# The first layer's inputs: x and ctx loaded ahead of the weights, the shift chunks taken in pairs, and two projection blocks accumulated tile by tile

## The chip, the cores and the metric

The kernel runs on one core of a Trainium2 chip. The metric is the device time of one execution in microseconds (us), a median over several runs. All times below are microseconds from the start of the profiled execution unless marked otherwise; PE is TensorE, DVE is VectorE, ACT is ScalarE, POOL is GpSimd, SP is SyncE, which here only issues transfers.

## The reference

The whole program is two networks one behind the other (a hybrid of a bidirectional recurrence and attention, MLPs, a state-space mixer, then a second block with three attention branches and a convolutional feed-forward). The change touches only the beginning of the first layer:

```python
mod_l = jnp.split((jax.nn.silu(c) @ ada_w[li] + ada_b[li])[:, None, :], 6, axis=-1)
mod_c = jnp.split(jax.nn.silu(c_ctx) @ ada_w[li] + ada_b[li], 6, axis=-1)
hl = rmsnorm(xl, norm1_g[li]) * (1.0 + mod_l[1]) + mod_l[0]
hc = rmsnorm(xc, norm1_g[li]) * (1.0 + mod_c[1]) + mod_c[0]
...
p_lat = h_lat @ w_in          # hybrid_mixer
p_ctx = h_ctx @ w_in
```

`x` (the latent stream) and `ctx` are 256 tokens by 1024 features each. `mod[0]` is the shift, `mod[1]` the scale; both come from a product of `silu(c)` with the first 2048 columns of `ada_w`.

## The kernel before

Features lie on partitions, tokens on the free axis: `xl` and `xc` are two tiles each of 128 x (4 x 256), and `xk` picks one of the eight k tiles (128 x 256). Both streams stand side by side in tiles of 512 columns, ctx first.

Weights come in blocks of 128 output columns: one load of 512 KB into a `raw` tile (128 x 1024, eight k tiles), issued on SP. A block is split into `whi` (rounded to fp32r, on ACT) and `wlo` (what is left, on DVE), the activation likewise into `hhi` and `hlo`; a projection (`projs`) is 24 matmuls of 512 columns into one PSUM bank: whi with hhi and with hlo for each k, then wlo with hhi for each k.

The modulation's first 16 chunks of 128 columns (`ada`, chunks 0 to 7 the shift, 8 to 15 the scale) are read by `adas`, four at a time: per chunk eight small matmuls against `scc` (the silu of c), then a copy out of PSUM (`adas`), a turn by transposes, a reduce and an add into `mod`.

`mod_act` in its `late` form made the activation: squares of x and ctx on ACT with their sums on PE (`stat`), the inverse root on DVE (`rsq`, ten small steps in a row), `spread` of the factor over the columns on PE, 16 multiplications of x and ctx by it on DVE, then all 16 chunks of `adas`, then for each k tile and stream `f = x*a + b` on DVE, `hhi` on ACT and `hlo = f - hhi` on DVE. With that the projections of the hybrid mixer begin: block 0 (the decay and a inputs), blocks 2 and 3 (the keys, `k`), and so on, each through `shifted`: `pp` copied out of PSUM on ACT, then `sm`, a scaled copy, and a sum on DVE. A second stream, `preps`, is woven between the projections (`weave`), and takes the keys as soon as a block is done.

Engines run their instructions in the order in which the tile framework's scheduler wrote them down; a wait at the head of an engine's queue holds up everything behind it. PSUM is cut into pools of banks by `banks`; `PS_PREP` is two banks of `mm` and six of `w`.

Of the kernel before, what the change touches and what calls it, by code (L numbers as in the profile page):

```python
# [16 lines left out]
T = 256  # L17
# [285 lines left out]
class Kern:  # L303
# [68 lines left out]
    def setup(self):  # L372
        nc, A = self.nc, self.A
        G = self.G = self.pool('G')
        self.ps, self.cut, self.sums, self.late = {}, None, None, []
        self.banks(mm=4, w=4)
        cc = self.tl(G, [128, 8, 2], 'cc')
        nc.sync.dma_start(cc, A['cc'])
        nv = sum(w for _, w in self.vc.values())
# [12 lines left out]
        self.W = self.pool('W')  # L392

    def load_x(self, P, Pc):
        self.xl = [self.tl(P, [128, 4, T], f'xl{i}') for i in range(2)]
# [43 lines left out]
    def projs(self, out, name, b, act, n0, n1):  # L439

        nc = self.nc
        whi, wlo = self.wsplit(self.wraw(name, b))
        ps = self.PSt('mm')[:, :n1 - n0]
        runs = [(w, a, k) for k in range(KT) for w, a in ((whi, act.hi), (whi, act.lo))]
        runs += [(wlo, act.hi, k) for k in range(KT)]
        for i, (w, a, k) in enumerate(runs):
            nc.tensor.matmul(ps, w[:, k], a[k][:, n0:n1], start=i == 0, stop=i == len(runs) - 1)  # L447
            if i % 6 == 5 and i < len(runs) - 1:
                yield 6 * (n1 - n0) / 2400
        out.append(ps)  # L450
        yield 6 * (n1 - n0) / 2400


    def adas(self, chunks, ring=None):

        nc = self.nc
        l = 0
        for b in chunks[::4]:
            ps = self.PSt('mm')
            if b < 16:  # L460
                raws = [self.wraw('ada', b + i, ring=ring) for i in range(4)]
                for i in range(4):
                    for r in range(2):
                        for g in range(4):
                            nc.tensor.matmul(ps[32 * g:32 * g + 32, 128 * i:128 * i + 128],
                                             self.scc[:, 2 * g + r], raws[i][:, 2 * g + r],
                                             start=r == 0, stop=r == 1)
                    yield 0.6
            else:
                raws = [self.wraw('adaw', (b // 4 - 4, g)).rearrange("p k c -> p (k c)") for g in range(4)]  # L470
                for r in range(2):
                    for g in range(4):
                        nc.tensor.matmul(ps[32 * g:32 * g + 32], self.scc[:, 2 * g + r],
                                         raws[g][:, 512 * r:512 * r + 512], start=r == 0, stop=r == 1)
                    yield 0.9
            sb = self.tl(self.W, [128, 512], 'adas', bufs=1)
            nc.scalar.activation(sb, ps, AF.Copy)
            yield 0.1
            pt = self.PSt('w')
            for i in range(4):  # L480
                nc.tensor.transpose(pt[:, 128 * i:128 * i + 128], sb[:, 128 * i:128 * i + 128],
                                    self.C('ident'))
            m = self.mod[l][:, b:b + 4]
            nc.vector.tensor_reduce(m, pt.rearrange("p (c g j) -> p c j g", c=4, g=4)[:, :, 0:2],
                                    AX.X, ADD)
            nc.vector.tensor_tensor(m, m, self.V(f'adab{l}')[:, b:b + 4, None].to_broadcast([128, 4, 2]),
                                    ADD)
            self.mods = b + 4
            yield 0.3

    def ada_rows(self, X):
# [111 lines left out]
            self.spread(pr[:, 128 * t:128 * t + 128], y[:, t:t + 1])  # L603
        return pr

    def mod_act(self, l, which, streams, P, X, mid=None, late=None):


        nc = self.nc
# [4 lines left out]
        pr = self.rms(xs, X, mid)  # L614
        cols = [(i, j, slice(T * i, T * i + T)) for i, j in enumerate(streams)]
        if late:
            for k in range(KT):
                for i, j, s in cols:
                    nc.vector.tensor_tensor(self.xk(xs[i], k), self.xk(xs[i], k), pr[:, s], MUL)
            late()  # L620
        m = 3 * which
        sc = {}
        for j in streams:
# [4 lines left out]
        for k in range(KT):  # L628
            for i, j, s in cols:
                x = self.xk(xs[i], k)  # L630
                a, b = sc[j][:, k:k + 1], self.mod[l][:, 8 * m + k, j:j + 1]
                f = self.tl(X, [128, T], 'mf', bufs=4)
                if late:
                    nc.vector.tensor_scalar(f, x, a, b, op0=MUL, op1=ADD)
                    nc.scalar.activation(hi[k][:, s], x, AF.Identity, scale=a, bias=b)
                    todo.append((lo[k][:, s], f, 0.0, hi[k][:, s]))
                else:
                    nc.vector.scalar_tensor_tensor(f, x, a, pr[:, s], op0=MUL, op1=MUL)
                    nc.scalar.activation(hi[k][:, s], f, AF.Identity, bias=b)
                    todo.append((lo[k][:, s], f, b, hi[k][:, s]))  # L640
# [30 lines left out]

    def hybrid(self):
        nc, A = self.nc, self.A
        R = self.pool('R', side='right')
        self.load_consts(1, R)
        self.Y = self.pool('Y', side='right')
        Hh = self.Hh = self.pool('Hh', side='right')
        X = self.pool('X0')
# [48 lines left out]
        self.R, self.DR = R, DR  # L727
# [1546 lines left out]
```

## Time and profile before

| | |
|---|---|
| median of 3 runs | 2044.55 us (2040.88 to 2045.95) |
| the profiled execution | 2040.4 us, span 2038.6 us |
| PE busy | 1938.1 us, 95% of the span |
| PE weight load busy | 1648.5 us, 81% |
| DVE busy | 1446.8 us, 71% |
| ACT busy | 964.4 us, 47% |
| POOL busy | 149.9 us, 7% |
| chain that ended last, by engine | PE 79%, DVE 8%, DMA 5%, issue 5%, ACT 2%, POOL 1% |

The span is what lies between the first and the last instruction of the profiled execution; its own time is 1.8 us longer. A busy PE counts matmuls whose ends are modelled and overlap, so it is no proof that PE runs at its peak. The part of the program that the change touches is the first 64 us of the span.

### The profile page before, as it was taken

To read this page: it belongs to the slowest core of one execution; us is meant where nothing else is said; L and a number is where in the kernel's file an instruction comes from. 1 tells how busy PE (TensorE), PEld (TensorE's weight loads), DVE (VectorE), ACT (ScalarE), POOL (GpSimd) and SP (SyncE) were. 2 spreads that over 40 slices of the span, in tenths; PEclk is the share of its full clock that TensorE was granted. 3 is DMA by queue.
4 is the path that set the end of the run, shared out by engine and by line. 5 is a ranking of instruction groups with operands and counts; after the bars stand their busy time and mean duration, and the time that the engine had idled before them with its cause. 6 is when DMAs were issued, how large, how long until landed. Compare 5 with 4: busy or idle time off the path is not lost.

```text
span 2038.6 us, 37380 instructions
## 1 busy us (share of the span) xinstructions
PE 1938.1 (95%) x14898; PEld 1648.5 (81%) x14898; DVE 1446.8 (71%) x3044; ACT 964.4 (47%) x1770; POOL 149.9 (7%) x273
## 2 busy tenths in 40 slices
PE   6999799969899999998999999999999999999999
PEld 4776456747698899986778878899986888899999
DVE  4675596696699854437988887666678666667984
ACT  3454233322552434434566665566655445456663
POOL 0022401201031200000000003000000000000000
PEclk8999898989899999999999999999999999999999
DMA  7355843413287853322223325466644323345664
GB/s 274 125 175 203 251 155 120 143 42 124 81 271 243 289 169 93 94 88 71 92 64 86 101 73 158 147 186 185 180 148 153 125 93 115 113 147 173 191 190 150
DMA packets 87021, 299.82 MB, mean 147 GB/s; under 512 B 11213, under 2 KB 14685, under 8 KB 86846
## 3 DMA queue, kind: packets, MB, share of 16 engines
q1 hardware_dynamic: 62064, 221.29, 34.1%
q0 software_dynamic: 20736, 69.64, 10.5%
q10 hardware_dynamic: 4046, 6.49, 1.0%
q8 instruction: 117, 1.92, 0.4%
q14 instruction: 58, 0.48, 0.1%
HBM read 281.63 MB, written 18.90 MB: 147 GB/s over the span
## 4 chain that ended last, share of the span: by engine, by line
PE 79%; DVE 8%; DMA 5%; issue 5%; ACT 2%; POOL 1%; POOLq 0%; SPq 0%; DVEq 0%; ACTq 0%
PE psmm L447 23%; PE psmm L426 11%; PE psmm L429 11%; PE psmm L427 11%; DMA ar<-adat 2%; PE psmm L1635 2%; PE psy L1698 2%; PE psw L524 1%; PE psw L1703 1%; DVE wlo L419 1%; PE psa L429 1%; PE psa L426 1%; PE psa L427 1%; PE pso L2054 1%; PE psya L972 1%
## 5 line engine op out<-in xcount | busy, mean ns | idle before, releaser
L418 ACT ACTIVATE whi<-raw 128x1024 fp32r<-128x1024 f32 x374 | 394.4, 1055 | 482.1 <-PE psmm L427 242.2
L419 DVE TENSOR_TENSOR wlo<-raw,whi 128x1024 fp32r<-128x1024 f32 x374 | 453.5, 1213 | 59.4 <-ACT whi L418 39.1
L447 PE MATMUL psmm<-hhi,whi 128*128 128x256 f32 (+1 forms) x1040 | 337.4, 346 | 6.5 <-ACT whi L418 2.1
L447 PE MATMUL psmm<-hlo,whi 128*128 128x256 f32 (+1 forms) x1040 | 330.9, 339 | 2.1 <-DVE hlo L665 1.5
L426 PE MATMUL psmm<-hhi,whi 128*128 128x258 f32 (+1 forms) x944 | 231.1, 283 | 0.3 <-ACT whi L418 0.3
L427 PE MATMUL psmm<-hlo,whi 128*128 128x258 f32 (+1 forms) x944 | 230.8, 282 | 0.0
L447 PEld LDWEIGHTS psmm<-hhi,whi 128*128 128x128 f32 x1040 | 199.8, 192 | 38.1 <-issue 12.2
L447 PEld LDWEIGHTS psmm<-hlo,whi 128*128 128x128 f32 x1040 | 199.7, 192 | 28.7 <-DVE hlo L663 4.8
L447 PE MATMUL psmm<-hhi,wlo 128*128 128x256 f32 (+1 forms) x1040 | 213.5, 336 | 0.2 <-DVE wlo L419 0.2
L426 PEld LDWEIGHTS psmm<-hhi,whi 128*128 128x128 f32 x944 | 178.7, 189 | 2.7 <-issue 1.4
L427 PEld LDWEIGHTS psmm<-hlo,whi 128*128 128x128 f32 x944 | 179.2, 190 | 0.7 <-issue 0.6
L447 PEld LDWEIGHTS psmm<-hhi,wlo 128*128 128x128 f32 x1040 | 157.4, 189 | 25.1 <-issue 9.1
L426 PE MATMUL psmm<-hi,whi 128*128 128x512 f32 (+1 forms) x512 | 164.0, 340 | 5.3 <-ACT hi L668 5.3
L427 PE MATMUL psmm<-lo,whi 128*128 128x512 f32 (+1 forms) x512 | 161.8, 336 | 0.0
L429 PE MATMUL psmm<-hhi,wlo 128*128 128x258 f32 (+1 forms) x944 | 132.0, 282 | 0.0
L429 PEld LDWEIGHTS psmm<-hhi,wlo 128*128 128x128 f32 x944 | 121.0, 190 | 0.0
L426 PEld LDWEIGHTS psmm<-hi,whi 128*128 128x128 f32 x512 | 96.4, 189 | 19.1 <-ACT hi L668 7.0
L511 DVE SCALAR_TENSOR_TENSOR aj<-ar,cb 128x1024 f32<-128x1024 f32 x80 | 97.8, 1222 | 13.2 <-DMA ar<-adat 10.2
L427 PEld LDWEIGHTS psmm<-lo,whi 128*128 128x128 f32 x512 | 96.3, 189 | 10.3 <-DVE lo L669 0.5
L429 PE MATMUL psmm<-hi,wlo 128*128 128x512 f32 (+1 forms) x512 | 100.0, 338 | 0.0
L1370 ACT ACTIVATE r<-r,s 128x256 f32<-128x256 f32 x96 | 48.9, 510 | 87.8 <-DVE r L1369 87.5
L429 PEld LDWEIGHTS psmm<-hi,wlo 128*128 128x128 f32 x512 | 81.6, 190 | 10.4
(607 smaller groups left out, 3649.0 us busy)
## 6 DMA issues: line engine op xcount, KB each, us to landing
raw<-w SPq DMA_DIRECT2D x128, 512.0 KB, 4.1
ar<-adat POOLq DMA_DIRECT2D x56, 512.0 KB, 4.9
raw<-win SPq DMA_DIRECT2D x55, 512.0 KB, 3.5
raw<-ssdin SPq DMA_DIRECT2D x49, 512.0 KB, 3.6
raw<-hyin SPq DMA_DIRECT2D x26, 512.0 KB, 4.1
raw<-adaw SPq DMA_DIRECT2D x24, 512.0 KB, 5.2
raw<-wg SPq DMA_DIRECT2D x22, 512.0 KB, 3.6
raw<-wu SPq DMA_DIRECT2D x22, 512.0 KB, 3.6
```

Of the source, the lines that this page charges most:

```text
L418: nc.scalar.activation(hi[:, :n], raw, AF.Copy)
L419: nc.vector.tensor_tensor(lo[:, :n], raw, hi[:, :n].bitcast(F32), SUB)
L426: nc.tensor.matmul(ps, whi[:, k], act.hi[k][:, n0:n1], start=start and i == 0, stop=False)
L427: nc.tensor.matmul(ps, whi[:, k], act.lo[k][:, n0:n1], start=False, stop=False)
L429: nc.tensor.matmul(ps, wlo[:, k], act.hi[k][:, n0:n1], start=False, stop=stop and i == len(ks) - 1)
L447: nc.tensor.matmul(ps, w[:, k], a[k][:, n0:n1], start=i == 0, stop=i == len(runs) - 1)
L511: nc.vector.scalar_tensor_tensor(junk, raw, 1.0, cb[j], op0=MUL, op1=MUL, accum_out=self.mod[l][:, b, j:j + 1])
L524: self.nc.tensor.matmul(out[32 * g:32 * g + 32, 128 * b:128 * b + 128], self.C('two' if heads else 'one'), sq, start=start, stop=stop, ski ...
L972: nc.tensor.matmul(pss[h][:, q], bk[r, q], ar[r, q], start=True, stop=True)
L1370: nc.scalar.activation(r[:, s], r[:, s], AF.Relu, bias=sh)
L1635: nc.tensor.matmul(ps, w[:, k0 + k], a[k], start=start and i == 0, stop=stop and i == len(runs) - 1, skip_group_check=True)
L1698: nc.tensor.matmul(o, w[:, q], m[:, q], start=d == 0 and n == 2 and q < 2 and k == 0, stop=k == 1 and d == 1 and n == 3, skip_group_check= ...
```

## The change

x and ctx are now issued first, on ACT's queue, ahead of the vectors and the constants. SP's queue takes the eight scale chunks first, then the weight blocks 0 and 2, then shift chunks with further weight blocks between them. The multiplication by the factor stays on DVE, the 16 `f = x*a + b` go from DVE to POOL, and the shift chunks are taken in pairs: after each pair the parts of its two k tiles are made and both blocks' matmuls of these k tiles (3 products by 2 tiles by 2 blocks) follow. Blocks 0 and 2 are finished in that way and `projs` only hands their PSUM banks over.

```diff
@@ setup
-        self.banks(mm=4, w=4)
+        self.banks(**self.PS_PREP)
         cc = self.tl(G, [128, 8, 2], 'cc')
         nc.sync.dma_start(cc, A['cc'])
...
+        self.load_x(self.X0, self.X0)
@@ wraw
-        raw = self.tl(ring, [128, KT, cols // KT], 'raw0', bufs=8) if ring else \
+        raw = self.tl(ring, [128, KT, cols // KT], f'raw{b // 8}', bufs=4 + b // 8 * 4) if ring else \
@@ projs
+        if (name, b) in self.early:
+            out.append(self.early.pop((name, b)))
+            yield 0.0
+            return
@@ adas
-        for b in chunks[::4]:
-            ps = self.PSt('mm')
+        for b in chunks[::n]:
+            ps = self.PSt('w' if b < 16 else 'mm')
...
+    def first_act(self, P, X, ring):
+        nc = self.nc
+        hi = [self.tl(P, [128, 512], 'hhi', F32R, bufs=KT) for _ in range(KT)]
+        lo = [self.tl(P, [128, 512], 'hlo', F32R, bufs=KT) for _ in range(KT)]
+        cols = [(self.xc, 1, slice(0, T)), (self.xl, 0, slice(T, 512))]
+        pr = self.rms([self.xc, self.xl], X)
+        for k in range(KT):
+            for xs, j, s in cols:
+                nc.vector.tensor_tensor(self.xk(xs, k), self.xk(xs, k), pr[:, s], MUL)
+        drain(self.adas(range(8, 16), ring=ring))
...
+        ws = [self.wsplit(self.wraw('hyin', b)) for b in (0, 2)]
+        pss = [self.PSt('mm') for _ in range(2)]
+        for k0 in range(0, KT, 2):
+            drain(self.adas(range(k0, k0 + 2), ring=ring, n=2))
+            for k in (k0, k0 + 1):
+                for xs, j, s in cols:
+                    x, a, b = self.xk(xs, k), sc[j][:, k:k + 1], self.mod[0][:, k, j:j + 1]
+                    f = self.tl(X, [128, T], 'mf', bufs=4)
+                    nc.gpsimd.tensor_scalar(f, x, a, b, op0=MUL, op1=ADD)
+                    nc.scalar.activation(hi[k][:, s], x, AF.Identity, scale=a, bias=b)
+                    nc.vector.tensor_tensor(lo[k][:, s], f, hi[k][:, s].bitcast(F32), SUB)
+                for (whi, wlo), ps in zip(ws, pss):
+                    for i, (w, a) in enumerate(((whi, hi), (whi, lo), (wlo, hi))):
+                        nc.tensor.matmul(ps, w[:, k], a[k], start=k + i == 0, stop=k == KT - 1 and i == 2)
+        for b, ps in zip((0, 2), pss):
+            self.early['hyin', b] = ps
+        return Act(hi, lo)
@@ hybrid
-        self.load_x(X, X)
-        act = self.mod_act(0, 0, [1, 0], Hh, X, late=lambda: drain(self.adas(range(16), ring=ring)))
+        act = self.first_act(Hh, X, ring)
```

Three places show how the engines' orders move. In all of them a number behind a name tells one tile from another.

The first is DVE, where the factor's inverse root (`rqv`, `rqt`, `rqy`) ends and the multiplications of `xc` and `xl` by the spread factor (`psw_207`) begin. Before:

```order
L562 SCALAR_TENSOR_TENSOR rqv_194<-rqt_196 128x4
L563 SCALAR_TENSOR_TENSOR rqy_195<-rqv_194,rqy_195 128x4
L619 TENSOR_TENSOR xc_103<-xc_103,psw_207 128x256
L619 TENSOR_TENSOR xl_101<-xl_101,psw_207 128x256
L619 TENSOR_TENSOR xc_103<-xc_103,psw_207 128x256
```

Now, with `raw_332` and `raw_338` the loads of blocks 0 and 2:

```order
L571 SCALAR_TENSOR_TENSOR rqv_194<-rqt_196 128x4
L424 TENSOR_TENSOR wlo_335<-raw_332,whi_334 128x1024
L572 SCALAR_TENSOR_TENSOR rqy_195<-rqv_194,rqy_195 128x4
L424 TENSOR_TENSOR wlo_341<-raw_338,whi_340 128x1024
L656 TENSOR_TENSOR xc_83<-xc_83,psw_207 128x256
L656 TENSOR_TENSOR xl_81<-xl_81,psw_207 128x256
```

The splits of two weight blocks now stand between the steps of the root and ahead of the multiplications, so the last step of the root waits for block 0's load.

The second is PE, from the spread of the factor (L568, L577) on. `psw_228` and `psw_278` hold the scale chunks, `psw_346` and `psw_402` the first two pairs of shift chunks, `psmm_344` and `psmm_345` blocks 0 and 2. Before, the spread stood among the chunks:

```order
L568 MATMUL psw_207<-cst_68,rqy_195 128x128 x4
L481 MATMUL psw_271<-cst_68,adas_269 128x128 x4
L465 MATMUL psmm_328<-raw_331,scc_70 32x128 x8
L481 MATMUL psw_321<-cst_68,adas_319 128x128 x4
L465 MATMUL psmm_328<-raw_333,scc_70 32x128 x8
```

Now all the chunks come behind it, and the products of a pair behind the next pair's chunks:

```order
L577 MATMUL psw_207<-cst_91,rqy_195 128x128 x4
L474 MATMUL psw_228<-raw_229,scc_93 32x128 x8
...
L490 MATMUL psw_369<-cst_91,adas_367 128x128 x2
L474 MATMUL psw_402<-raw_403,scc_93 32x128 x8
L474 MATMUL psw_402<-raw_405,scc_93 32x128 x8
L675 MATMUL psmm_344<-hhi_109,whi_334 128x512
L675 MATMUL psmm_345<-hhi_109,whi_340 128x512
L675 MATMUL psmm_344<-hlo_117,whi_334 128x512
...
L675 MATMUL psmm_345<-hhi_110,wlo_341 128x512
L490 MATMUL psw_425<-cst_91,adas_423 128x128 x2
```

The transposes that turn the next pair (`psw_425`) stand behind the twelve products of this pair.

The third is ACT, where blocks 0 and 2 are copied out of PSUM (`pp`) and block 3's weights are rounded (`whi_641`, now `whi_645`). Before:

```order
L713 ACTIVATE pp_592<-psmm_567 128x2x256
L418 ACTIVATE whi_641<-raw_639 128x1024
L418 ACTIVATE whi_679<-raw_677 128x1024
L713 ACTIVATE pp_632<-psmm_607 128x2x256
L747 ACTIVATE wt_540<-wdad_539 64x512
L739 ACTIVATE x_691<-k_541,vec_66 128x512
```

Now:

```order
L742 ACTIVATE pp_627<-psmm_344 128x2x256
L742 ACTIVATE pp_636<-psmm_345 128x2x256
L423 ACTIVATE whi_645<-raw_643 128x1024
L423 ACTIVATE whi_683<-raw_681 128x1024
L776 ACTIVATE wt_614<-wdad_613 64x512
L768 ACTIVATE x_695<-k_615,vec_89 128x512
```

Block 3's weights are now rounded behind both copies. On PE, the statistics of the squared keys (`x_691`, now `x_695`) stood after block 3's twentieth matmul and now stand after its ninth. From block 3's end on, each engine's order is that of before, but for one transpose.

## Rows read from the trace of the kernel before

**Rows 1.** Busy time by stretch: engines' busy time (instructions), granted PE clock, DMA share, GB/s.

```profile
0.00:22.20 22.20, 9.08 (x134) 5.92 (x134) 0.71 (x5) 5.13 (x13) 1.39 (x9) 1.00 0.93 354
39.00:49.20 10.20, 9.29 (x17) 4.70 (x18) 10.20 (x31) 8.06 (x16) 0.25 (x1) 0.50 0.00 1
63.80:140.00 76.20, 76.16 (x362) 57.86 (x361) 54.80 (x112) 37.85 (x63) 14.17 (x34) 1.00 0.42 143
```

**Rows 2.** Transfers of the first 36 us: queues (packets, MB), one issuing line (KB each).

```profile
q10 hardware_dynamic: 1008, 2.88, 22.1%
q0 software_dynamic: 80, 0.26, 1.8%
...
raw<-ada SPq DMA_DIRECT2D x16, 512.0 KB, 9.5
```

**Rows 3.** Timeline, 27 to 36 us: start, duration, engine, line, operation [idle before].

```profile
27.73 0.16 DVE L563 SCALAR_TENSOR_TENSOR rqy<-rqv,rqy 128x4 f32<-128x4 f32 x1
27.94 0.65 PE L568 MATMUL psw<-cst,rqy 128*128 128x128 f32 x4 [1.46 <-DVE rqy L563]
28.69 0.42 DVE L619 TENSOR_TENSOR xc<-xc,psw 128x256 f32<-128x256 f32 x1 [0.80 <-PE psw L568]
29.22 1.08 PE L465 MATMUL psmm<-raw,scc 128*32 128x128 f32 x16
32.84 0.60 ACT L477 ACTIVATE adas<-psmm 128x512 f32<-128x512 f32 x1 [2.85 <-PE psmm L465]
33.49 0.65 PE L481 MATMUL psw<-cst,adas 128*128 128x128 f32 x4 [0.79 <-ACT adas L477]
33.66 0.41 DVE L619 TENSOR_TENSOR xl<-xl,psw 128x256 f32<-128x256 f32 x1
34.08 1.95 PE L465 MATMUL psmm<-raw,scc 128*32 128x128 f32 x64
```

**Rows 4.** Timeline, 37 to 40 us: the first parts of the activation.

```profile
37.73 0.17 DVE L486 TENSOR_TENSOR mod<-mod,vec 128x8 f32<-128x8 f32 x1
38.13 0.60 ACT L635 ACTIVATE hhi<-xc,mod,msc 128x256 fp32r<-128x256 f32 x1 [0.43 <-DVE msc L625]
39.27 0.80 PE L447 MATMUL psmm<-hhi,whi 128*128 128x512 f32 x1 [1.81 <-ACT hhi L635]
```

**Rows 5.** Lines by form, 20 to 50 us: busy us, mean ns of one.

```profile
L663 DVE TENSOR_TENSOR hlo<-mf,hhi 128x256 fp32r<-128x256 f32 x16 | 6.6, 423 | 0.0
...
L418 ACT ACTIVATE whi<-raw 128x1024 fp32r<-128x1024 f32 x2 | 2.1, 1046 | 0.0
...
L419 DVE TENSOR_TENSOR wlo<-raw,whi 128x1024 fp32r<-128x1024 f32 x1 | 1.2, 1228 | 0.0
```

**Rows 6.** Timeline, 48 to 64 us: from the last low-clock products to block 3's end.

```profile
48.26 0.63 PE L447 MATMUL psmm<-hlo,whi 128*128 128x512 f32 x1
48.69 0.59 PE L447 MATMUL psmm<-hhi,whi 128*128 128x512 f32 x1
54.02 0.60 ACT L713 ACTIVATE pp<-psmm 128x512 f32<-128x512 f32 x1 [6.96 <-PE psmm L447]
54.65 0.69 DVE L715 TENSOR_TENSOR sm<-pp 128x512 f32<-128x512 f32 x1 [3.12 <-ACT pp L713]
58.05 0.48 DVE L717 TENSOR_SCALAR k<-pp,omm 128x512 f32<-128x512 f32 x1
59.59 0.75 DVE L718 SCALAR_TENSOR_TENSOR k<-sm,hm,k 128x512 f32<-128x512 f32 x1
61.30 0.41 PE L524 MATMUL psw<-x,cst 128*32 128x128 f32 x4
63.73 0.39 PE L447 MATMUL psmm<-hhi,whi 128*128 128x512 f32 x1
63.96 0.39 PE L447 MATMUL psmm<-hlo,whi 128*128 128x512 f32 x1
```

**Rows 7.** Lines by form of POOL: its only arithmetic on tiles of this size.

```profile
L1317 POOL COPY xc<-df 128x256 f32<-128x256 f32 x4 | 1.5, 406 | 0.0
```

More of the change, by code (lines that the diff above doesn't have):

```diff
@@ L374, in setup @@
         G = self.G = self.pool('G')
-        self.ps, self.cut, self.sums, self.late = {}, None, None, []
-        self.banks(mm=4, w=4)
+        self.ps, self.cut, self.sums, self.late, self.early = {}, None, None, [], {}
+        self.banks(**self.PS_PREP)
         cc = self.tl(G, [128, 8, 2], 'cc')
         nc.sync.dma_start(cc, A['cc'])
+        self.W = self.pool('W')
+        self.R = self.pool('R', side='right')
+        self.Y = self.pool('Y', side='right')
+        self.Hh = self.pool('Hh', side='right')
+        self.X0 = self.pool('X0')
+        self.load_x(self.X0, self.X0)
         nv = sum(w for _, w in self.vc.values())
@@ L391, in setup @@
         nc.gpsimd.memset(self.mod[1], 0.0)
-        self.W = self.pool('W')
     def load_x(self, P, Pc):
@@ L451, in projs, with adas @@
         yield 6 * (n1 - n0) / 2400
-    def adas(self, chunks, ring=None):
+    def adas(self, chunks, ring=None, n=4):
         nc = self.nc
         l = 0
-        for b in chunks[::4]:
-            ps = self.PSt('mm')
+        for b in chunks[::n]:
+            ps = self.PSt('w' if b < 16 else 'mm')
             if b < 16:
-                raws = [self.wraw('ada', b + i, ring=ring) for i in range(4)]
-                for i in range(4):
+                raws = [self.wraw('ada', b + i, ring=ring) for i in range(n)]
+                for i in range(n):
                     for r in range(2):
@@ L476, in adas @@
             sb = self.tl(self.W, [128, 512], 'adas', bufs=1)
-            nc.scalar.activation(sb, ps, AF.Copy)
+            nc.scalar.activation(sb[:, :128 * n], ps[:, :128 * n], AF.Copy)
             yield 0.1
             pt = self.PSt('w')
-            for i in range(4):
+            for i in range(n):
                 nc.tensor.transpose(pt[:, 128 * i:128 * i + 128], sb[:, 128 * i:128 * i + 128],
                                     self.C('ident'))
-            m = self.mod[l][:, b:b + 4]
-            nc.vector.tensor_reduce(m, pt.rearrange("p (c g j) -> p c j g", c=4, g=4)[:, :, 0:2],
+            m = self.mod[l][:, b:b + n]
+            nc.vector.tensor_reduce(m, pt[:, :128 * n].rearrange("p (c g j) -> p c j g", c=n, g=4)[:, :, 0:2],
                                     AX.X, ADD)
-            nc.vector.tensor_tensor(m, m, self.V(f'adab{l}')[:, b:b + 4, None].to_broadcast([128, 4, 2]),
+            nc.vector.tensor_tensor(m, m, self.V(f'adab{l}')[:, b:b + n, None].to_broadcast([128, n, 2]),
                                     ADD)
-            self.mods = b + 4
+            self.mods = b + n
             yield 0.3
@@ L604, in rms, with mod_act @@
         return pr
-    def mod_act(self, l, which, streams, P, X, mid=None, late=None):
+    def mod_act(self, l, which, streams, P, X):
         nc = self.nc
@@ L613, in mod_act @@
         xs = [(self.xl, self.xc)[j] for j in streams]
-        pr = self.rms(xs, X, mid)
+        pr = self.rms(xs, X)
         cols = [(i, j, slice(T * i, T * i + T)) for i, j in enumerate(streams)]
[L616 to L620, printed above, removed]
         m = 3 * which
@@ L632, in mod_act @@
                 f = self.tl(X, [128, T], 'mf', bufs=4)
[L633 to L640, printed above, removed]
+                nc.vector.scalar_tensor_tensor(f, x, a, pr[:, s], op0=MUL, op1=MUL)
+                nc.scalar.activation(hi[k][:, s], f, AF.Identity, bias=b)
+                todo.append((lo[k][:, s], f, b, hi[k][:, s]))
                 if len(todo) > 2:
@@ L644, in mod_act @@
             self.low(*t)
+        return Act(hi, lo)
[9 more added lines that the diff above has]
+        drain(self.adas(range(8, 16), ring=ring))
+        sc = [self.tl(X, [128, 8], f'msc{j}') for j in range(2)]
+        for j in (1, 0):
+            nc.vector.scalar_tensor_tensor(sc[j], self.mod[0][:, 8:16, j], 1.0, self.V('n1g0'), op0=ADD, op1=MUL)
+        ws = [self.wsplit(self.wraw('hyin', b)) for b in (0, 2)]
[14 more added lines that the diff above has]
+            self.early['hyin', b] = ps
         return Act(hi, lo)
@@ L673, in hybrid @@
         nc, A = self.nc, self.A
-        R = self.pool('R', side='right')
+        R, Hh, X = self.R, self.Hh, self.X0
         self.load_consts(1, R)
-        self.Y = self.pool('Y', side='right')
-        Hh = self.Hh = self.pool('Hh', side='right')
-        X = self.pool('X0')
         ring = self.pool('A0')
-        self.load_x(X, X)
-        act = self.mod_act(0, 0, [1, 0], Hh, X, late=lambda: drain(self.adas(range(16), ring=ring)))
+        act = self.first_act(Hh, X, ring)
         ring.release()
@@ L726, in hybrid @@
         self.bonus = [self.tl(R, [128, 512], f'bon{p}') for p in range(4)]
-        self.R, self.DR = R, DR
+        self.DR = DR
         sig = self.sig = self.tl(R, [128, 512], 'sig')
```

## The prediction

> **What bounds the kernel now.** I first read the busy time by stretch. From 63.8 to 140 us PE is busy for 76.16 of 76.20 us at the full clock [rows 1]: behind the beginning the projections keep PE full, so whatever the change gains or loses at the beginning should be passed on to the end, one for one. Then I read the beginning itself in the timeline, to find what PE waits for. Until 22.2 us the loads run at 354 GB/s, 7.86 MB in all [rows 1]; of these and the next 14 us, ACT's queue (x, ctx, vectors, constants) carries 2.88 MB, POOL's 0.26, and a chunk or a weight block is 512 KB, 0.52 MB [rows 2]. The modulation is whole at 37.9 us [rows 4], and from then to 49 us the activation's parts are made: DVE is busy for 10.20 of 10.20 us between 39.0 and 49.2, PE fills the time with two matmuls per k tile, and its granted clock is 0.50 of full, the lower of its two levels, 1.2 GHz [rows 1]. In that stretch a product starts 0.43 us after the one before it (48.26 to 48.69); at the full clock it is 0.23 (63.73 to 63.96) [rows 6]. Block 3 ends, and the block after it begins, at 63.73 [rows 6]. From there on both programs have the same order, so 63.73 is the mark against which I set the changed kernel: its time at this mark, less 63.73, is the change.
>
> **The first step: the factor.** Bytes that must land before block 0's weights: 2.88 MB of ACT's queue, 0.26 of POOL's, eight scale chunks and the block itself, 9 x 0.524 = 4.72; the sum is 7.86 MB, which the trace had moved by 22.2 us [rows 1, 2]. By the new order of DVE, block 0's split stands ahead of the root's last step. The rounding on ACT takes 1.05 and the split 1.23 [rows 5], so the root ends at 22.2 + 1.05 + 1.23 + 0.2 = 24.7 and the spread starts at 24.9, against 27.94 before [rows 3]. That is the lower end. The constants that the sums need now stand behind x and ctx in ACT's queue, and if the sums end no sooner than before, the spread starts at 27.94 plus a split, 29.2. I take 25.9, nearer the lower end, since x itself comes sooner. The 16 multiplications (28.69 to 33.66 and 0.41: 5.4 us [rows 3]) then end at about 32.3 behind block 2's split; they lie beside PE's chunks, below, and cost nothing as long as these take longer.
>
> **The second step: the chunks.** All of them now stand behind the spread on PE. It takes 0.65; the scale's 64 matmuls take 1.95 us as the last 64 did, or 4 x 1.08 = 4.3 at the pace of the 16 at 29.22; the two copies and turns 0.60 + 0.65 + 0.2 between engines, 1.45 each [rows 3]. The first pair adds 16 matmuls (0.5 to 1.1), a smaller copy and turn (0.8), reduce and add (0.4). From the spread's end that is 6.6 to 9.5 us; with 25.9 + 0.65 I get 33.1 to 36.1 and take 34.3, in the middle. So the first two k tiles can start 3.6 us before 37.9. The loads of the third and fourth pairs wait for ring tiles that the first and second free at about 33 to 34; at 0.52 MB per 1.3 us they land by about 39, ahead of their turn, and cost nothing unless a pair takes under 2.5 us.
>
> **The third step: a pair.** From `mod` to the first product PE waited 1.14 us (38.13 to 39.27 [rows 4]). Then twelve products: 12 x 0.23 = 2.8 at the full clock, 5.2 at the low one. The next pair's turn stands behind them on PE: 0.2 for the last product to leave, 0.3 for two transposes, 0.6 for reduce, add and two hand-overs. A pair takes 5.0 us at the full clock and 7.4 at the low one; the last, with no turn behind it, 4.1 or 6.5. I take the first at 6.6 (it starts behind small matmuls with gaps) and the others at the full clock: 6.6 + 5.0 + 5.0 + 4.1 = 20.7. Blocks 0 and 2 end at 34.3 + 20.7 = 55.0. The bounds are 33.1 + 19.1 = 52.2 with the full clock throughout, and 36.1 + 28.7 = 64.8 with the low one.
>
> Here the parts `f` are new on POOL. The nearest row is a copy of the same shape, 0.41 us [rows 7]; I take 0.5. Bounds: 0.41 for one pass, 0.8 for two passes, one for each of the two operations. Four of them must end 1.7 us before the pair's products do (`hlo` 0.42 [rows 5], a hand-over, five products), at 2.3 us in a pair at the full clock. So 0.5 is hidden with 0.3 us to spare in a pair, and 0.8 would cost 4 x 0.8 - 2.3 = 0.9 a pair, 3.6 in all.
>
> **The fourth step: the tail.** Before, the copies of blocks 0 and 2 out of PSUM lay beside products. Now both blocks end together, at E. Block 0's copy starts 0.55 before E (three products of block 2 come last), block 2's at E + 0.2, each 0.6; only then is block 3's weight rounded (1.05 [rows 5]), and PE starts block 3 at E + 1.95. On DVE the keys follow: 0.63 from the copy to the first `sm` (54.02 to 54.65), two `sm` of 0.69, two scaled copies of 0.48, a sum of 0.75, block 3's split 1.23, then the key's own sum, which led to the first statistic on PE 1.71 us after it began (59.59 to 61.30 [rows 5, 6]). Less 0.4 of overlap between neighbours that is E + 5.7. PE does nine products (2.1) up to E + 4.05 and stands for 1.65 us. Behind it come the statistics (0.9 with their changes) and 15 products (3.45): block 3 ends at E + 10.05. Of this 3.6 us are new idle time, which nothing covers.
>
> **The sum.** 55.0 + 10.05 = 65.05 against 63.73: 1.3 us later. The profiled execution took 2040.4, which makes 2041.7; the median of the three runs stands 4.15 above that execution, so I forecast 2044.55 + 1.3 = 2045.9. What the change gains (3.6 us sooner at the first pair, and products that no longer wait for DVE's `f`) it gives back in the turns between pairs, and in the tail.
>
> **A rule of the skill.** No row of before shows DVE with two inputs of 256 columns from SBUF beside POOL reading SBUF. The Trainium skill, SBUF — State Buffer, section Who interferes with whom, says that a DVE instruction with two SBUF inputs contends with a GpSimd instruction that reads SBUF, and that the second to issue waits for the first. `hlo` is such an instruction. By that rule the four `hlo` and four `f` of a pair would queue, and the sum would be the first rival's, below; by the copy's row alone it stays at 65.05.
>
> **The rivals.** *POOL becomes the bound.* Place: `f` in each pair. If three `hlo` of 0.42 [rows 5] stand between four `f` of 0.5, the last `f` ends 3.3 us after `mod` instead of 2.0, 1.0 beyond the 2.3 that is hidden: 4 x 1.0 = 4 us, 2050. With `f` at 0.8 it is 4 x 2.2 = 8.7 us, 2054.6. It decides (slower by over 6.1 us) when an `f` and its waits together take 0.88 us: (2.3 + (6.1 - 1.3) / 4) / 4. For it: sixteen new instructions in a loop through four engines. Against: the copy's 0.41.
>
> *PE stays at the low clock through the pairs.* In before it did so for 10.2 us while its products came in twos with waits between them [rows 1]. 36.1 + 28.7 + 10.05 = 74.85, 11.1 us later than the mark: 2055.7; with the chunks in my middle, 2053.9. Against it: twelve products in a row at the low clock fill 5.2 of 7.4 us, more than before's two in each k tile.
>
> *Faster after all.* With the spread at 24.9, the chunks at 6.6, and the full clock throughout, E is 32.1 + 19.1 = 51.2, block 3 ends at 61.3, 2.5 us sooner: 2042.1. Beyond 6.1 us it gets only if the tail's 3.6 us vanish as well, at 2038.5. For it: all of this lies within my bounds. Against: the tail hangs on written orders, not on chance.
>
> **How the numbers follow.** A difference under 0.3%, 6.1 us, can't be told from none by a measurement of this kernel. My forecast, within that: 0.58, between 2040 and 2050. POOL as the bound: 0.20, of which 0.13 lies beyond 6.1 us. The low clock: 0.12, nearly all beyond. Faster: 0.08, and 0.02 more for something in later stages that I don't see. Together: faster by over 0.3% 0.10, the same 0.65 (0.58 and POOL's smaller case, 0.07), slower 0.25. The range, 8 in 10, goes from 2039, near the faster end with a hidden tail, to 2055, between the two slow cases.
>
> **What the profile would show.** The spread at 25 to 27 us and block 0's split just ahead of it; the first `hhi` at 33 to 36; pairs 5 to 7 us apart, their `f` at 0.4 to 0.6; blocks 0 and 2 ending at 52 to 58; PE idle for some 1.9 us before block 3 and 1.6 in it; block 3's end at 62 to 68. I am wrong if the chunks run before the spread on the chip, if a pair takes under 4.4 us, if an `f` takes over 0.8, or if the mark and the end of the program move by different amounts.

## The result, and the profile after

The changed kernel took 2055.09 us (median of 11 runs, 2047.20 to 2060.61), the kernel before 2044.03 beside it (11 runs, 2035.72 to 2051.48). The ratio is 1.0062 with a 95% interval of 1.0041 to 1.0083: slower, by 11 us of median, where 1.3 us were forecast; the median lies just above the range's upper end of 2055. Its profiled execution took 2057.93 us, with a span of 2056.1.

The mark, block 3's end and the start of the next block, moved from 63.73 [rows 6] to 75.25, by 11.5 us. The first view is the busy time by stretch, cut at the prediction's steps; its columns are those of [rows 1].

```profile
0.00:22.20 22.20, 3.73 (x40) 1.96 (x40) 0.62 (x5) 5.29 (x14) 1.30 (x7) 1.00 0.91 347
22.20:42.50 20.30, 14.79 (x224) 10.72 (x224) 10.38 (x36) 5.54 (x12) 0.00 (x0) 0.75 0.58 224
42.50:65.50 23.00, 18.81 (x142) 11.62 (x130) 8.91 (x30) 9.71 (x20) 12.27 (x19) 0.93 0.36 124
65.50:75.25 9.75, 6.84 (x33) 4.84 (x33) 6.00 (x9) 4.80 (x6) 0.21 (x2) 1.00 0.51 153
75.25:151.50 76.25, 76.21 (x362) 57.99 (x361) 54.75 (x112) 38.01 (x63) 14.62 (x34) 1.00 0.42 143
```

In the first 22.2 us PE is now busy for 3.73 us, against 9.08 before, while the loads run at much the same rate, 347 against 354 GB/s [rows 1]: the chunks that PE took as they landed have gone to the next stretch. From the mark on PE is full again, 76.21 of 76.25 us, so nothing is won back there.

The second view is the timeline, from the sums of squares to the first `mod` (start, duration, engine, line, operation, and the idle time before with what ended it).

```profile
18.33 6.57 PE L533 MATMUL psw<-sq,cst 128*32 128x128 f32 x64 [18.33 <-DMA cst<-cst]
25.70 0.16 DVE L562 TENSOR_SCALAR rqv<-psw 128x4 f32<-128x4 f32 x1 [7.17 <-PE psw L551]
...
27.37 1.23 DVE L424 TENSOR_TENSOR wlo<-raw,whi 128x1024 fp32r<-128x1024 f32 x1
28.51 0.15 DVE L572 SCALAR_TENSOR_TENSOR rqy<-rqv,rqy 128x4 f32<-128x4 f32 x1
28.72 1.11 PE L577 MATMUL psw<-cst,rqy 128*128 128x128 f32 x4 [3.06 <-DVE rqy L572]
29.77 3.64 PE L474 MATMUL psw<-raw,scc 128*32 128x128 f32 x64
34.12 1.12 PE L490 MATMUL psw<-cst,adas 128*128 128x128 f32 x4 [0.72 <-ACT adas L486]
35.17 3.44 PE L474 MATMUL psw<-raw,scc 128*32 128x128 f32 x64
39.40 0.66 PE L490 MATMUL psw<-cst,adas 128*128 128x128 f32 x4 [0.79 <-ACT adas L486]
42.31 0.16 DVE L495 TENSOR_TENSOR mod<-mod,vec 128x4 f32<-128x4 f32 x1
```

The sums wait for the constants, which now come behind x and ctx; block 0's split stands in the root; then the scale chunks come in two groups of 64 records, 3.64 and 3.44 us, with a copy and a turn behind each. The granted clock from 22.2 to 42.5 is 0.75 in the mean.

The third is the timeline of the pairs and of the tail.

```profile
42.52 0.60 ACT L670 ACTIVATE hhi<-xc,mod,msc 128x256 fp32r<-128x256 f32 x1 [0.94 <-DVE mod L495]
42.59 0.55 POOL L669 TENSOR_SCALAR mf<-xc,msc,mod 128x256 f32<-128x256 f32 x1 [40.61 <-DVE mod L495]
44.62 0.82 POOL L669 TENSOR_SCALAR mf<-xl,msc,mod 128x256 f32<-128x256 f32 x1
44.67 0.43 DVE L671 TENSOR_TENSOR hlo<-mf,hhi 128x256 fp32r<-128x256 f32 x1 [0.38 <-POOL mf L669]
48.04 0.60 ACT L670 ACTIVATE hhi<-xc,mod,msc 128x256 fp32r<-128x256 f32 x1 [3.18 <-DVE mod L495]
53.73 0.60 ACT L670 ACTIVATE hhi<-xc,mod,msc 128x256 fp32r<-128x256 f32 x1 [3.35 <-DVE mod L495]
59.39 0.60 ACT L670 ACTIVATE hhi<-xc,mod,msc 128x256 fp32r<-128x256 f32 x1 [3.31 <-DVE mod L495]
64.43 0.63 PE L675 MATMUL psmm<-hlo,whi 128*128 128x512 f32 x1
64.85 0.63 PE L675 MATMUL psmm<-hhi,wlo 128*128 128x512 f32 x1
66.01 2.00 ACT L423 ACTIVATE whi<-raw 128x1024 fp32r<-128x1024 f32 x2
67.11 0.50 PE L456 MATMUL psmm<-hhi,whi 128*128 128x512 f32 x1 [1.63 <-ACT whi L423]
70.78 0.42 PE L533 MATMUL psw<-x,cst 128*32 128x128 f32 x6 [1.30 <-ACT x L768]
75.25 0.39 PE L456 MATMUL psmm<-hhi,whi 128*128 128x512 f32 x1
```

The pairs come 5.52, 5.69 and 5.66 us apart (42.52, 48.04, 53.73, 59.39), each ended by a wait of ACT for the next `mod`. An `f` takes 0.55 us alone and mostly 0.80 to 0.82 (0.97 once) when `hlo` run beside it. The last products start 0.42 us apart, the low clock's spacing [rows 6]. Blocks 0 and 2 end at 65.48, and the tail to the mark takes 9.77 us with both waits that were forecast, 1.63 for block 3's `whi` and 1.30 in it.

### The profile page after: what moved, and what is told of

Read it like the earlier page. It is cut to its first block, busy times and chain, and to the rows that moved or that the text cites. A ratio compares the mean times of both kernels' runs of the same rounds, so it can differ in the third digit from the quotient of the medians.

```text
span 2056.1 us, 37395 instructions
## 1 busy us (share of the span) xinstructions
PE 1944.4 (95%) x14898; PEld 1652.7 (80%) x14898; DVE 1444.0 (70%) x3032; ACT 964.9 (47%) x1772; POOL 162.0 (8%) x289
## 4 chain that ended last, share of the span: by engine, by line
PE 77%; DVE 9%; issue 5%; DMA 3%; ACT 2%; POOL 1%; ACTq 0%; POOLq 0%; DVEq 0%
PE psmm L456 22%; PE psmm L431 11%; PE psmm L432 10%; PE psmm L434 10%; PE psmm L1664 2%; PE psy L1727 2%; DVE aj L520 2%; DMA ar<-adat 1%; DVE wlo L424 1%; PE psw L533 1%; PE psw L1732 1%; PE psa L434 1%; PE psa L431 1%; PE psa L432 1%; PE pso L2083 1%
## 5 line engine op out<-in xcount | busy, mean ns | idle before, releaser
L456 PE MATMUL psmm<-hhi,whi 128*128 128x256 f32 (+1 forms) x1024 | 329.4, 343 | 6.3 <-ACT whi L423 3.7
L456 PE MATMUL psmm<-hlo,whi 128*128 128x256 f32 (+1 forms) x1024 | 322.3, 336 | 1.5 <-DVE hlo L698 1.5
L456 PEld LDWEIGHTS psmm<-hhi,whi 128*128 128x128 f32 x1024 | 195.5, 191 | 38.2 <-issue 11.8
L456 PEld LDWEIGHTS psmm<-hlo,whi 128*128 128x128 f32 x1024 | 195.7, 191 | 23.8 <-issue 5.0
L456 PE MATMUL psmm<-hhi,wlo 128*128 128x256 f32 (+1 forms) x1024 | 207.8, 333 | 0.0
L431 PEld LDWEIGHTS psmm<-hhi,whi 128*128 128x128 f32 x944 | 178.7, 189 | 2.7 <-issue 1.4
L432 PEld LDWEIGHTS psmm<-hlo,whi 128*128 128x128 f32 x944 | 179.0, 190 | 0.7 <-issue 0.6
```

The source lines that it names most:

```text
L431: nc.tensor.matmul(ps, whi[:, k], act.hi[k][:, n0:n1], start=start and i == 0, stop=False)
L432: nc.tensor.matmul(ps, whi[:, k], act.lo[k][:, n0:n1], start=False, stop=False)
```

## The experiments

The theory (A): the loss is made before the mark and passed on one for one; most of it stands between the spread and the first `mod` (what became of this is told behind the table), where scale chunks that used to run while loads were landing now run behind the factor; the rest is a late spread and pairs that are longer than forecast. Rivals: (B) the pairs make the loss, by POOL and by PE's turns; (C) the mark doesn't pass to the end, and the loss lies further down; (D) the low clock of one execution makes it.

**1. The scale chunks ahead of the factor.**

```diff
+        drain(self.adas(range(8, 16), ring=ring))
         pr = self.rms([self.xc, self.xl], X)
...
-        drain(self.adas(range(8, 16), ring=ring))
```

> The eight scale chunks are taken ahead of the factor, as their loads land; all else as in the changed kernel. Theory A (the loss at the mark of 11.5 us is made at the beginning, and most of it by the 7.1 us of scale chunks that stand behind the spread): the first mod of a shift pair follows the spread within 3 us instead of 13.75, the spread itself comes later than 28.72, at 31 to 33, since the sums now stand behind the eighth chunk; the first hhi starts at 33 to 38 instead of 42.52, block 3 ends at 67 to 71 instead of 75.25, and the time is 4 to 8 us under that of the changed kernel, 2047 to 2051. Theory B (the loss is made in the pairs, by POOL and PE's turns): the pairs start sooner but take that much longer, and block 3 ends within 2 us of 75.25. Theory C (the mark doesn't pass to the end): block 3 ends sooner and the time stays within 2 us of the changed kernel's.

Measured: 2055.75 us, ratio 1.0067 (1.0044 to 1.0091). The timeline around the factor:

```profile
23.60 1.95 PE L474 MATMUL psw<-raw,scc 128*32 128x128 f32 x64
...
35.10 0.62 PE L577 MATMUL psw<-cst,rqy 128*128 128x128 f32 x4 [2.13 <-DVE rqy L572]
...
40.73 0.41 DVE L657 TENSOR_TENSOR xl<-xl,psw 128x256 f32<-128x256 f32 x1
41.06 0.24 DVE L493 TENSOR_REDUCE mod<-psw 128x4 f32<-128x16 f32 x2
...
41.46 0.60 ACT L670 ACTIVATE hhi<-xc,mod,msc 128x256 fp32r<-128x256 f32 x1 [0.99 <-DVE mod L495]
```

From the spread to the first `hhi` 6.4 us are left of 13.8. That is A's direction, but the first `mod` follows the spread by 6.2 us, not by 3: the sixteen multiplications by the factor hold it, as its reduce stands behind the last of them on DVE (41.06), while PE had turned the pair by 38.4. The spread itself went to 35.10: the sums, now behind the chunks on PE, end at 32.2 instead of 24.9, and the first `hhi`, the mark (71.72) and the time are above what was expected. The sixth run puts the chunks among the sums instead. The time did not follow the mark's 3.5 us; the interval is as wide as that, so this run decides nothing on C.

**2. The constants ahead of x and ctx.**

```diff
-        self.load_x(self.X0, self.X0)
         nv = sum(w for _, w in self.vc.values())
...
         self.load_consts(0, G)
+        self.load_x(self.X0, self.X0)
```

> The vectors and the first constants are issued ahead of x and ctx on ACT's queue; all else as in the changed kernel. Theory A: the sums on PE, which waited for the constants until 18.33, start at 11 to 15, the spread starts at 24.5 to 26.5 instead of 28.72 (no sooner, as block 0's split stands ahead of the root's last step), and everything up to block 3's end moves by the same 2 to 4 us: 71 to 73 instead of 75.25, and the time is 2 to 4 us under the changed kernel's. Theory B (the order of the loads costs nothing, since the chunks bind): the spread moves, the first hhi stays within 0.5 us of 42.52.

Measured: 2050.53 us, ratio 1.0036 (1.0019 to 1.0054). The spread starts at 25.61, and the first `mod` at 36.65, 11.04 later; the mark is 69.58. The spread moved by 3.1 us, within the 2 to 4 expected, and everything up to the mark with it; B's outcome, a first `hhi` that stays, did not come (36.84). The mark is under the 71 to 73 expected: the other 2.6 us there are the two groups of chunks, which took 3.04 and 1.96 us instead of 3.64 and 3.44:

```profile
25.61 1.12 PE L577 MATMUL psw<-cst,rqy 128*128 128x128 f32 x4 [3.61 <-DVE rqy L572]
26.65 3.04 PE L474 MATMUL psw<-raw,scc 128*32 128x128 f32 x64
31.00 1.96 PE L474 MATMUL psw<-raw,scc 128*32 128x128 f32 x64
```

The length of the first group, and of the spread ahead of it (1.12, against 0.65 in [rows 3]), is that of the low clock, yet this profile has the granted clock at 1.00 from 22 to 33 us: here the rows show the pace, and its cause stays open.

**3. `f` on DVE again.**

```diff
-                    nc.gpsimd.tensor_scalar(f, x, a, b, op0=MUL, op1=ADD)
+                    nc.vector.tensor_scalar(f, x, a, b, op0=MUL, op1=ADD)
```

> The sixteen parts f are made on DVE again; all else as in the changed kernel. If POOL's f (0.55 alone, 0.80 to 0.82 beside hlo of DVE) binds the pairs: they come 5.0 to 5.2 us apart instead of 5.5 to 5.7, block 3 ends 1.5 to 2.5 us sooner, at 72.8 to 73.8, and the time falls by as much. If the turn on PE binds them, or DVE with eight steps of 0.42 a pair takes POOL's place: the pairs stay within 0.2 us, and the mark within 1 us of 75.25.

Measured: 2054.73 us, ratio 1.0055 (1.0031 to 1.0079). The pairs' first `hhi` start at 39.84, 44.91, 50.26 and 55.33, 5.07, 5.35 and 5.07 us apart: about 0.5 us a pair is POOL's, as the first outcome has it. The mark came at 70.75, more than this explains; the first `hhi` alone, which the edit doesn't touch, was 2.7 us sooner. The median is 0.4 us under the changed kernel's, so the time did not fall with the mark.

**4. The kernel before, with x and ctx first.** The part of the change in `setup` that issues x and ctx ahead of the vectors and constants, alone.

> The kernel before, with one part of the change alone: x and ctx issued ahead of the vectors and the constants on ACT's queue. Theory A (x first makes the constants late, and the sums with them): the sums start at 18 instead of 17.7 and are packed with chunks, the spread starts at 27.5 to 30 against 27.94, the modulation is whole at 38 to 42 against 37.9, block 3 ends at 64 to 68 against 63.73, and the time is 0 to 4 us over that of the kernel before. Rival (x first helps by itself): the spread starts 1 us or more before 27.94 and block 3 ends before 63.

Measured: 2047.33 us, ratio 1.0022 (1.0003 to 1.0042). The spread started at 29.14, the last `mod` at 40.09, and the mark came at 67.44: 3.7 us later than before. A's outcome: this part of the change costs by itself. In the spread it costs 1.2 us; the rest comes behind it and was not traced to a cause.

**5. The next pair's turn ahead of this pair's products.**

```diff
+        drain(self.adas(range(2), ring=ring, n=2))
         for k0 in range(0, KT, 2):
-            drain(self.adas(range(k0, k0 + 2), ring=ring, n=2))
+            if k0 + 2 < KT:
+                drain(self.adas(range(k0 + 2, k0 + 4), ring=ring, n=2))
```

> Only the place of a pair's turn is changed: each pair's chunks, copy, transposes, reduce and add are written ahead of the products of the pair before it. The first hhi should stay where it was in the changed kernel or in its versions, 39.8 to 42.5. If the turn behind the twelve products sets the length of a pair (5.5 to 5.7 us), the pairs now come as fast as POOL makes four f of 0.81, 3.3 us apart, blocks 0 and 2 end some 7 us sooner, block 3 ends at 66 to 68.5 instead of 75.25, and the time is 6 to 9 us under that of the changed kernel. If POOL's f or the products set it, the pairs stay over 5 us and block 3's end moves by under 2 us.

Measured: 2050.31 us, ratio 1.0017 (0.9997 to 1.0037). The pairs' first `hhi` are 3.5 to 4.2 us apart, and the mark is at 69.75:

```profile
40.70 0.60 ACT L672 ACTIVATE hhi<-xc,mod,msc 128x256 fp32r<-128x256 f32 x1 [0.93 <-DVE mod L495]
44.20 0.60 ACT L672 ACTIVATE hhi<-xc,mod,msc 128x256 fp32r<-128x256 f32 x1 [1.15 <-DVE mod L495]
48.12 0.60 ACT L672 ACTIVATE hhi<-xc,mod,msc 128x256 fp32r<-128x256 f32 x1 [1.04 <-DVE mod L495]
52.35 0.60 ACT L672 ACTIVATE hhi<-xc,mod,msc 128x256 fp32r<-128x256 f32 x1 [1.05 <-DVE mod L495]
```

The turn on PE does hold the pairs; without it they come a little slower than POOL's 3.3. The mark missed the upper end by 1.25 us: blocks 0 and 2 ended at 57.4, but the tail took 12.4 us.

**6. The scale chunks among the sums.** The constants as in the second run; `rms` takes one step of the scale chunks' generator behind each k tile's sums.

```diff
                 self.settle()
+                next(side, None)
...
-        pr = self.rms([self.xc, self.xl], X)
+        side = self.adas(range(8, 16), ring=ring)
+        pr = self.rms([self.xc, self.xl], X, side=side)
+        drain(side)
...
-        drain(self.adas(range(8, 16), ring=ring))
```

> The beginning alone is put in order: constants ahead of x and ctx as in the second run, and the eight scale chunks written among the sums of squares, one behind every k tile; f stays on POOL and the pairs as they are written. With that the order also brings three pairs' chunks ahead of the first products. Theory A (the 13.75 us from the spread to the first mod were chunks that ran too late): the spread starts at 25 to 28, the first pair's mod is there within 4 us, the first hhi at 29 to 33, the parts are then made at POOL's pace, 16 f of 0.81 in 13 us, block 3 ends at 54 to 60, that is 4 to 10 us before the mark of the kernel before, and the time is 3 to 9 us under that of the kernel before. Rival (the loads of the shift chunks come too late to gain): the first product waits for the seventh shift chunk until 38 or later, and block 3 ends at 63 to 68.

Measured: 2052.07 us, ratio 1.0028 (1.0008 to 1.0048). A miss: the spread came at 29.76, the mark at 66.93. The rival's two figures came (the first product started at 40.43), but PE waited for the shift chunks' loads for 0.4 us only. The sums ended at 21.6, but block 0's rounding stood ahead of the sums' copy on ACT and waited for its load, and its split stood ahead of the root on DVE:

```profile
24.45 1.06 ACT L423 ACTIVATE whi<-raw 128x1024 fp32r<-128x1024 f32 x1 [3.32 <-DMA raw<-hyin]
25.42 0.26 ACT L545 ACTIVATE tu<-psw 128x128 f32<-128x128 f32 x1
```

**7 and 8. The beginning and the pairs together**, with the splits written behind the first pair's chunks, eight ring tiles, and `f` on DVE (7) or on POOL (8).

> The sixth run's beginning, the next pair's chunks ahead of a pair's products, eight ring tiles for the shift chunks so that no load waits for one, the split of blocks 0 and 2 written behind the first pair's chunks, and f on DVE. First hhi at 29 to 33, all 48 products in a row behind the last shift chunk, 36 to 38, at the full clock 11 us: blocks 0 and 2 end at 47 to 50, block 3 at 57 to 60 against 63.73 before, the time 2038 to 2041. Rival (the beginning doesn't bind the whole program): block 3 ends that much sooner and the time stays within 2 us of that of the kernel before.

> The seventh run with f on POOL. If POOL's f at 0.81 beside hlo matters once nothing else holds the pairs: 16 f take 13 us from the first mod, the last hlo comes at 44 to 46, and block 3 ends 0 to 3 us later than in the seventh run. If DVE with f and hlo (16 times 0.33 and 16 times 0.33 from start to start, 10.6 us, behind the sixteen multiplications) is no faster: block 3 ends at the same time within 0.5 us or sooner.

Measured: 2047.47 us, ratio 1.0008 (0.9992 to 1.0025), and 2045.89 us, 0.9997 (0.9981 to 1.0014). The marks came at 64.64 and 64.50, the spread at 30.03 and 30.23, for the same reason as in the sixth run: written later, the splits were still ahead of the root in the order. The seventh run is a miss, with its first `hhi` at 40.18; in the eighth the second outcome came: with the pairs' chunks ahead, `f` costs the same on either engine.

**9. The changed kernel again.**

> The changed kernel once more, with nothing edited. Its first profile shows the eight scale chunks at the low clock (3.64 and 3.44 us for four) and the last pair at the low clock too, where the second, third and fifth runs' show 1.7 to 2.0 us for the second four. If these stretches belong to the kernel: the first hhi at 42 to 43 and block 3's end at 74.5 to 76 again. If they belong to the one execution: the first hhi at 39.5 to 41, block 3's end at 71 to 73.5, and some 2 to 3 us of the 11.5 at the mark are the profiled execution's own. The median of the times stays at 2053 to 2057 in either case.

Measured: 2057.73 us, ratio 1.0047 (1.0028 to 1.0066). The spread at 28.28, the first `mod` at 39.91, the first `hhi` at 40.11, the mark at 72.83. The second outcome came, but for a median 0.7 us above its range: 2.4 of the 11.5 us at the mark belong to the first execution (D in that part), and 9.1 remain. The low clock is not that execution's alone: the first group of chunks took 3.64 us in both, the second 3.44 and 1.95. This execution's spread, first `mod` and mark, and its windows, cut as above:

```profile
28.28 1.11 PE L577 MATMUL psw<-cst,rqy 128*128 128x128 f32 x4 [3.05 <-DVE rqy L572]
39.91 0.16 DVE L495 TENSOR_TENSOR mod<-mod,vec 128x4 f32<-128x4 f32 x1
72.83 0.39 PE L456 MATMUL psmm<-hhi,whi 128*128 128x512 f32 x1
...
22.20:40.10 17.90, 12.39 (x223) 8.92 (x224) 10.29 (x36) 5.35 (x11) 0.00 (x0) 0.81 0.66 251
40.10:62.80 22.70, 17.53 (x142) 10.85 (x130) 8.82 (x29) 9.54 (x20) 12.27 (x19) 1.00 0.36 124
62.80:72.83 10.03, 8.22 (x33) 5.92 (x33) 6.08 (x9) 4.96 (x7) 0.21 (x2) 0.83 0.54 155
```

The pairs ran at the full clock here and the tail partly at the low one; in the first profile it was the other way round.

**10 and 11. Blocks 0 and 2 loaded and split behind the first four shift chunks**, otherwise as 8 and 7; the edit against these:

```diff
-        wr = [self.wraw('hyin', b) for b in (0, 2)]
...
-        ws = [self.wsplit(w) for w in wr]
...
+            if k0 == 0:
+                ws = [self.wsplit(self.wraw('hyin', b)) for b in (0, 2)]
```

> The eighth run, with one thing moved: blocks 0 and 2 are loaded behind the first four shift chunks, and split there, so that their split no longer stands ahead of the root's first step on DVE and their rounding no longer ahead of the sums' copy on ACT. In the eighth run the sums ended at 21.8 and the spread came at 30.2. If that order alone held it: the spread starts at 24 to 26.5, the first hhi at 31.5 to 34 against 38.2, the f take 13 us at POOL's pace, block 3 ends at 55 to 59 against 64.5, and the time is 2035 to 2041, under that of the kernel before. If the loads hold it: the first hhi moves by under 2 us and block 3 ends at 62 to 65.

> The tenth run with f on DVE. DVE then has 16 multiplications, two splits, 16 f and 16 hlo in a row: 5.4 + 2.5 + 10.6 us from the spread on; block 3 ends within 1.5 us of the tenth run's, and the time within 2 us.

Measured: 2045.83 us, ratio 0.9995 (0.9979 to 1.0012), and 2047.19 us, 1.0007 (0.9991 to 1.0022). The root is free now:

```profile
21.73 0.28 ACT L545 ACTIVATE tu<-psw 128x128 f32<-128x128 f32 x1 [0.51 <-PE psw L533]
...
24.48 0.65 PE L577 MATMUL psw<-cst,rqy 128*128 128x128 f32 x4 [0.73 <-DVE rqy L572]
...
31.50 1.22 DVE L424 TENSOR_TENSOR wlo<-raw,whi 128x1024 fp32r<-128x1024 f32 x1
31.69 2.50 POOL L674 TENSOR_SCALAR mf<-xc,msc,mod 128x256 f32<-128x256 f32 x1 [29.71 <-DVE mod L495]
31.95 0.58 ACT L675 ACTIVATE hhi<-xc,mod,msc 128x256 fp32r<-128x256 f32 x1
32.70 1.22 DVE L424 TENSOR_TENSOR wlo<-raw,whi 128x1024 fp32r<-128x1024 f32 x1
...
62.11 0.39 PE L456 MATMUL psmm<-hhi,whi 128*128 128x512 f32 x1
```

Spread and first `hhi` came where they were expected, 5.7 and 7.3 us sooner than in the eighth run, but the mark moved by 2.4 us only, to 62.11 (62.80 with `f` on DVE): at the mark and in the time this is a miss, and the mark lies where the rival had it, though the first `hhi` does not. The gain went to the first `f`, 2.50 us beside the two splits on DVE; to the fourth pair, whose chunks stand behind the second pair's products on PE (`hhi` of the third pair at 37.98, of the fourth at 44.46); and to the tail, 12.6 us from the last product's end at 49.49. This is the best order found. It ends 1.6 us ahead of the kernel before at the mark, and its time can't be told from that kernel's.

**The mark and the end.** Set against each other, in us over the kernel before (the mark of one profiled execution each, and the ratio times 2044.5):

| run | mark | time | | run | mark | time |
|---|---|---|---|---|---|---|
| changed | +11.5 | +12.7 | | 5 | +6.0 | +3.5 |
| changed again | +9.1 | +9.6 | | 6 | +3.2 | +5.7 |
| 1 | +8.0 | +13.7 | | 7 | +0.9 | +1.6 |
| 2 | +5.9 | +7.4 | | 8 | +0.8 | -0.6 |
| 3 | +7.0 | +11.2 | | 10 | -1.6 | -1.0 |
| 4 | +3.7 | +4.5 | | 11 | -0.9 | +1.4 |

A straight line through the twelve has a slope of 1.12. Each time is uncertain by some 4 us, and in eleven of the twelve the interval holds the mark's figure; in the first run it misses it by 1 us. The `memset` of `S` on POOL, at 215.57 before and 227.29 in the changed kernel, moved by 11.7 us; over all these profiles it lies 151.8 to 152.3 us behind the mark. So C is excluded up to 216 us. Behind that point one execution differs from the next by several us: from the mark to the span's end it is 1974.9 us in the profile of before, 1980.9 in that of the changed kernel, and 1970.0 in the changed kernel's second. In ten of the twelve it is 1978.2 to 1984.8. Runs 7, 8, 10 and 11 are among these with times like the kernel before's, so the one profile of before, of an execution 4 us under its median, is likely short by itself; a loss of a few us behind 216 us isn't excluded for the changed kernel.

**Where the loss lies.** From the start to the spread, from there to the first `mod` (in the kernel before the last `mod`, as no part is made ahead of it), and from there to the mark, in us:

| | to the spread | to `mod` | to the mark |
|---|---|---|---|
| before [rows 3, 4, 6] | 27.94 | 9.79 | 26.00 |
| changed | 28.72 | 13.59 | 32.94 |
| changed again | 28.28 | 11.63 | 32.92 |

The loss is 0.8 + 3.8 + 6.9 us in the first execution and 0.3 + 1.8 + 6.9 in the second. So what A says of the mark and the end holds, and its "most of it" does not: the chunks behind the spread are the largest part of what the forecast missed, but the larger part of the loss against the kernel before lies behind the first `mod`, as B has it, in the pairs and the tail. The same stretch takes 32.93 us in the second run, 31.11 in the third (`f` on DVE) and 29.24 in the fifth (turns ahead).

## Why the prediction was wrong, point by point

The forecast had the mark at +1.3 us, and the two executions of the changed kernel +11.5 and +9.1.

- *What bounds the kernel*: right. PE is full behind the mark, and the change at the mark is passed on to the time, within what the medians can tell.
- *The factor*: forecast 25.9, measured 28.72 and 28.28, near the upper bound of 29.2, for the reason that the bound gave: constants behind x and ctx, and a split inside the root. The second run took the first away and got 25.61; the fourth shows it without the rest, as 1.2 us in the spread. The choice of the lower end was wrong by 2.4 to 2.8 us.
- *The chunks*: **the step that failed.** From the spread's start to the first `mod` 8.4 us were forecast; 13.6 and 11.6 were measured, and 11.0 to 11.9 in the second, third and fifth runs. The prediction counted "the scale's 64 matmuls" once at 1.95 us, but a chunk leaves 16 records in the trace (the row at 29.22 in [rows 3] is one chunk), so a row of 64 is four chunks and the eight need two of them. That second group took 1.95 to 3.44 us; the two copies and turns had been counted. The first pair's two chunks leave 32 records, 1.08 us, where 0.5 to 1.1 were counted. The rest is pace: a group took 1.95 us at the full clock and 3.64 at the low one. And the bound of 9.5 us, with its low-clock pace for one group only, was no upper bound. The mechanism, all chunks serial behind the spread, was right; the term was mis-sized by 5.2 us in the first profile, half of the whole miss, and by 3.2 in the second. (That the multiplications cost nothing holds only while the chunks take longer, as the prediction said: in the first run they hold the first `mod`.)
- *A pair*: 20.7 us forecast from `mod` to the last product's end, 23.2 and 22.1 measured. The first pair was shorter than forecast (5.5 against 6.6), the next two longer (5.7 against 5.0), and the last the most: 6.3, in part at the low clock (0.50 from 63 to 65.5 us), and 5.2, against 4.1. The turn behind the products holds the pairs, as forecast: the fifth run took it away and brought the pairs to 3.5 to 4.2. `f` was taken at 0.5 and measured 0.82, the upper bound, which the third run prices at 0.5 us a pair.
- *The tail*: 10.05 forecast, 9.77 and 10.81 measured. Right, with both waits; in the tenth run, where PE stands 2.45 us before it and the granted clock is 0.60 from 52 to 58 us, it is 12.6.
- *The sum*: +2.8 from the factor, +5.2 from the chunks, +2.5 from the pairs, -0.3 from the tail make +10.2 on the forecast 1.3, the measured 11.5. In the second execution it is +2.4, +3.2, +1.4 and +0.8, which makes 9.1.
- *The rivals*: POOL as the bound was right in its mechanism (the last `f` of the first pair ends 3.1 us after `mod`; forecast 3.3) and worth some 2 us instead of 4 (20.1 us from `mod` to the last product's end in the third run, 22.1 in the second execution); why not 4 was not tried. The low clock came in part: 0.93 in the mean of the pairs in one execution, 1.00 in the other. The argument given against it does not stand: in the kernel before PE was busy for 9.29 of the 10.20 us at the low clock [rows 1], a larger share than 5.2 of 7.4, so that the low clock mostly stayed away is luck as far as that argument goes. The faster case did not come; its place, a spread at 24.9 and quick chunks, is what the tenth run built, and even there the pairs and the tail ate it. Of the signs of being wrong one came, narrowly: an `f` over 0.8.

The prediction put the rule where it bears: the Trainium skill, SBUF — State Buffer, section Who interferes with whom, has the second of the two instructions wait. The trace agrees in kind: `f` went from 0.55 to 0.82 beside an `hlo`, and `f` to `f` is 0.81. It doesn't show which of the two issued first: the record of `f` at 44.62 begins 0.05 us ahead of that of `hlo`, and it is `f` that is longer, while `hlo` keeps its 0.43.

Open is how much of the residues in the table (5.7 us in the first run, 4.2 in the third) is chance. What decides which of PE's stretches runs at the low clock in an execution was not tried. Nor were the PSUM banks, which the change cuts otherwise in `setup`, tried by themselves.

## What to carry to other kernels

Work that ran while loads were landing cost nothing here; before such work is moved behind a dependency, count it at its full length, in units that one row of the trace proves (how many records a chunk leaves). A load put first puts others last (the constants landed at 18.2 us instead of 5.7), so look for the smallest tile that the first computation needs, here the constants. And in engines that run in written order, a split or a rounding that waits for a load must not stand inside a latency chain: the same splits, moved behind it with their loads, gave the factor back 5.7 us.

## What the runs showed of the hardware that was not expected

A POOL `f` of 128x256 with two scalars per partition took 0.55 us alone, 0.82 beside one `hlo` of DVE, and 2.50 beside two splits of 128x1024 (1.22 us each). Four scale chunks took 1.95 us or 3.64: from 29.7 to 35.2 us the granted clock was 0.50 in the changed kernel's first profile, 0.66 in its second and 1.00 in the second run's, where PE had been busy for 3.73, 3.92 and 7.69 of the first 22.2 us. A granted clock of 1.00 did not always go with the full pace: in the second run 64 records took 3.04 us at it. The time of one kernel spread by 10 to 25 us over its runs, as much as the largest of these edits moved the mark.
